# Half of h transposed by a trip through HBM and by VectorE, in a decoder layer on one core

## The chip, the cores and the metric

The kernel runs on 1 core of a Trainium2 chip. The metric is the device time of one launch in microseconds. Every time below is of the kernel before the change unless it is said otherwise.

## What is computed

One layer of a hybrid decoder: 256 tokens, width 2048, inner width 8192, all in float32. Two kinds of attention stand side by side; their heads are joined and projected back, and an MLP follows. The change touches only the passage between the last two.

```python
        mixed = jnp.concatenate([a_out.reshape(B, S, DSWA_HEADS * HEAD_DIM),
                                 b_out.reshape(B, S, MLA_HEADS * V_HEAD_DIM)], axis=-1)
        x = x + _rmsnorm(mixed @ w_out[layer], norm_attn_post[layer])

        h = _rmsnorm(x, norm_mlp_pre[layer])
        u = jnp.square(jax.nn.relu(h @ w_up[layer]))
        x = x + _rmsnorm(u @ w_down[layer], norm_mlp_post[layer])
```

Here `x` is 256 x 2048, `w_out` is 2048 x 2048, `w_up` 2048 x 8192 and `w_down` 8192 x 2048.

## The kernel before

**Numbers.** A float32 product is made from three products in a reduced type: each operand is split into `hi` (rounded, by ScalarE) and `lo` (the rest, by VectorE), and TensorE adds hi·hi, lo·hi and hi·lo. The helper `split` issues the two instructions; `split_gain` does the same and multiplies each row by its gain. So each tile of weights goes from HBM to `raw` (by SyncE's queue), then to `hi` (ScalarE), `lo` (VectorE), and to TensorE. There are 5 buffers for `raw` and 8 pairs `hi`, `lo`.

**Tokens and tiles.** The 256 tokens are two blocks of 128, block 0 and block 1. In a matmul the 128x128 stationary tile is taken from the transposed activations (rows of it are the 128 values of k over which the sum runs, columns are the tokens) and 512 columns of weights stream past. So h has to be turned: `hT` holds 16 tiles k of 128 rows, 256 tokens each, as `hT_hi` and `hT_lo`.

**From w_out to w_up.** The products with w_out are made in three passes over its columns, 512 columns to an accumulator `acc_o`. `out_evac` takes an accumulator out: ScalarE squares it (`junko`), VectorE multiplies by the gain into `yg`. When the last 512 columns of block b are there, the chain `residual(b)` starts:

- VectorE sums the squares, POOL takes the power (`rstd_post`, L506), and VectorE adds the scaled `yg` to `x` in four updates of 512 columns (`x0` and `x1` for the two blocks, L960).
- TensorE turns 512 columns at a time, in groups of four 128x128 transposes into a PSUM bank (`ht0` to `ht3`, L308). ScalarE and VectorE split each group into `hT_hi` and `hT_lo` (L314, L315). `parts[b]` counts the groups; the matmuls of tile k are put into the program only when the groups up to it are (`h_done`).
- POOL stores x in HBM with four DMAs (`xkeep`, L976). It is read again at the end of the layer.
- ScalarE takes the squares of the new x (`junkx`, L980, four of 512 columns), VectorE sums them, POOL makes `rstd_pre2`, which scales the result of w_up later. So the transposed h is the unscaled x; its gain is in the weights (`gcol`).

**The first chunk of w_up.** w_up is worked through in 8 chunks of 1024 columns; the first one (j = 0) is plain: 16 tiles of weights, 2 blocks, 2 halves of 512 columns, 3 products, hence 6 matmuls per tile and block into `acc_u0_<block><half>`. Tile k of this chunk is weight 119 + k (`hi119` is k = 0, `hi127` k = 8, `hi132` k = 13). Its order is written out: block 0 for k = 0 to 6, then block 1 for k = 0 to 6, then from k = 7 both blocks in turn.

```python
        order = in_order(len(steps), (APART[1], 0)) if j == 0 else [(t, b) for t, (w, _, _) in enumerate(steps)
        for t, b in order:
            if (j, t, b) == (0, 8, 0):
                flow.finish(*res)
                late["po"].release()
```

At (0, 8, 0), block 0 at k = 8, both residual chains have to be wholly in the program. Then the pool `po` is given back, which held `x0`, `x1`, `yg0`, `yg1` and `junk`, and in its place the pool `up` is made, with `ab`, `ab2`, `c` and others. The next chunks use products on sums of tiles; `all_sums` makes the sums of hT in `c` (with `left_sums`, on VectorE and ScalarE), and POOL and SyncE load pairs of tiles of w_up into `ab` and `ab2`. Later `c` also receives the turned inner activations.

**What sets the order.** All instructions of an engine run in the order of the program. The order is made at build time by a small planner, `Flow`: a chain such as `residual` yields a number of planned microseconds before its next piece, matmuls advance the planned clock by their cost (`flow.spend`), and `flow.pump` emits the pieces that are due. `flow.until` and `flow.finish` advance the planned clock to what they need. `D_NORM`, `D_HT` and `D_SECOND` are such delays: before the first transposes, between groups, and between the starts of the two chains.

## Time and profile before

| what | value |
|---|---|
| time, median of 3 runs | 1021.92 us (1021.72 to 1022.56) |
| the profiled execution: its time, its span | 1022.2 us, 1020.4 us |
| granted TensorE clock, mean over the span | 0.997 |
| busy: PE, PEld, DVE, ACT, POOL | 1009.9, 842.3, 841.4, 625.0, 101.1 us |
| matmuls (records) | 4670 |
| HBM read, written | 232.64 MB, 33.56 MB |
| passage concerned: last w_out products to k = 8 of both blocks | about 336 to 368 us |

PE is TensorE's matmuls, PEld its loads of stationary tiles, which overlap them; DVE is VectorE, ACT is ScalarE, POOL is GpSimd, SP is SyncE. The span goes from the first to the last instruction of the profiled execution; the time of a run also holds what lies around it. In a row of the timeline stand the start, the duration, the engine, the line of the kernel, the operation, the output and the inputs, and in brackets how long the engine had been idle before and what ended that. A row of POOLq, ACTq or SPq is a DMA being issued by that engine. Rows of DMA issues give the number, the size and the median time from issue to landing.

### The profile page before, as it was taken

To read this page: it belongs to the slowest core of one execution; us is meant where nothing else is said; L and a number is where in the kernel's file an instruction comes from. 1 tells how busy PE (TensorE), PEld (TensorE's weight loads), DVE (VectorE), ACT (ScalarE), POOL (GpSimd) and SP (SyncE) were. 2 spreads that over 40 slices of the span, in tenths; PEclk is the share of its full clock that TensorE was granted. 3 is DMA by queue.
4 is the path that set the end of the run, shared out by engine and by line. 5 is a ranking of instruction groups with operands and counts; after the bars stand their busy time and mean duration, and the time that the engine had idled before them with its cause. 6 is when DMAs were issued, how large, how long until landed. Compare 5 with 4: busy or idle time off the path is not lost.

```text
span 1020.4 us, 13299 instructions
## 1 busy us (share of the span) xinstructions
PE 1009.9 (99%) x4670; PEld 842.3 (83%) x4670; DVE 841.4 (82%) x1127; ACT 625.0 (61%) x824; POOL 101.1 (10%) x160
## 2 busy tenths in 40 slices
PE   9999999999999999999999999999999999999996
PEld 6888889898888788888888888888888888888885
DVE  6676747676666679998999989897999998898985
ACT  6575436555454567576766776676666665767661
POOL 0020302102101200000010100000110000211100
PEclk9999999999999999999999999999999999999998
DMA  8977759656687477777988979679989867888952
GB/s 291 371 250 261 245 166 309 217 175 185 207 310 208 173 298 245 258 256 241 301 264 278 286 222 295 200 253 352 338 271 391 290 234 259 296 304 333 367 187 82
DMA packets 109170, 267.07 MB, mean 262 GB/s; under 512 B 9520, under 2 KB 28464, under 8 KB 108464
## 3 DMA queue, kind: packets, MB, share of 16 engines
q1 hardware_dynamic: 65584, 175.14, 50.0%
q0 software_dynamic: 20144, 71.31, 21.1%
q10 hardware_dynamic: 23376, 19.78, 6.2%
q8 instruction: 36, 0.59, 0.2%
q14 instruction: 30, 0.25, 0.1%
HBM read 232.64 MB, written 33.56 MB: 261 GB/s over the span
## 4 chain that ended last, share of the span: by engine, by line
PE 95%; DVE 2%; issue 1%; DMA 1%; ACT 0%; POOL 0%; DVEq 0%; POOLq 0%; SPq 0%; ACTq 0%
PE acc_u L304 26%; PE y L304 25%; PE acc_o L304 8%; PE md L304 6%; PE m L304 6%; PE acc_v L304 5%; PE acc_qk L304 4%; PE acc_q L304 3%; PE acc_k L304 3%; PE acc_ckv L304 3%; PE acc_cq L304 2%; PE sc_b L304 1%; DMA raw<-in_w_in 1%; PE acc_qr L304 1%; PE y L1346 1%
## 5 line engine op out<-in xcount | busy, mean ns | idle before, releaser
L315 DVE TENSOR_TENSOR lo<-raw,hi 128x1024 fp32r<-128x1024 f32 (+2 forms) x205 | 233.4, 1157 | 65.5 <-ACT hi L314 64.1
L314 ACT ACTIVATE hi<-raw 128x1024 fp32r<-128x1024 f32 (+2 forms) x205 | 202.7, 1004 | 75.1 <-DMA raw<-in_w_in 21.8
L304 PE MATMUL acc_u<-hi,hT_lo 128*128 128x512 f32 x386 | 150.4, 390 | 0.4 <-DVE hT_lo L315 0.4
L304 PE MATMUL acc_u<-hi,hT_hi 128*128 128x512 f32 x386 | 150.7, 390 | 0.0
L304 PE MATMUL acc_u<-lo,hT_hi 128*128 128x512 f32 x386 | 150.2, 389 | 0.0
L304 PE MATMUL y<-hi,ulo 128*128 128x512 f32 x358 | 139.3, 389 | 0.0
L304 PE MATMUL y<-lo,uhi 128*128 128x512 f32 x358 | 139.3, 389 | 0.0
L304 PE MATMUL y<-hi,uhi 128*128 128x512 f32 x358 | 139.3, 389 | 0.0
L318 ACT ACTIVATE hi<-raw,gcol 128x1024 fp32r<-128x1024 f32 x86 | 96.7, 1148 | 32.6 <-PE acc_u L304 16.1
L319 DVE SCALAR_TENSOR_TENSOR lo<-raw,gcol,hi 128x1024 fp32r<-128x1024 f32 x86 | 106.5, 1272 | 9.1 <-ACT hi L318 9.1
L304 PEld LDWEIGHTS acc_u<-hi,hT_lo 128*128 128x128 f32 x386 | 72.4, 188 | 15.8 <-DVE hT_lo L315 0.9
L304 PEld LDWEIGHTS acc_u<-lo,hT_hi 128*128 128x128 f32 x386 | 72.5, 188 | 15.0
L304 PEld LDWEIGHTS acc_u<-hi,hT_hi 128*128 128x128 f32 x386 | 72.5, 188 | 14.9
L304 PEld LDWEIGHTS y<-lo,uhi 128*128 128x128 f32 x358 | 67.2, 188 | 14.1
L304 PEld LDWEIGHTS y<-hi,uhi 128*128 128x128 f32 x358 | 67.2, 188 | 14.0
L304 PEld LDWEIGHTS y<-hi,ulo 128*128 128x128 f32 x358 | 67.2, 188 | 13.9
L315 DVE TENSOR_TENSOR lo<-st_down,hi 128x1024 fp32r<-128x1024 f32 x46 | 55.0, 1218 | 0.8 <-ACT hi L314 0.8
L304 PE MATMUL acc_o<-hi,mixT_hi 128*128 128x512 f32 x128 | 51.3, 401 | 0.0
L314 ACT ACTIVATE hi<-u 128x1024 fp32r<-128x1024 f32 (+1 forms) x33 | 32.3, 980 | 30.3 <-PE y L304 12.1
L304 PE MATMUL acc_o<-hi,mixT_lo 128*128 128x512 f32 x128 | 49.9, 390 | 0.0
L304 PE MATMUL md<-hi,s 128*128 128x512 f32 x138 | 49.9, 389 | 0.0
L304 PE MATMUL acc_o<-lo,mixT_hi 128*128 128x512 f32 x128 | 49.8, 389 | 0.0
(356 smaller groups left out, 2046.9 us busy)
## 6 DMA issues: line engine op xcount, KB each, us to landing
raw<-in_w_up SPq DMA_DIRECT2D x86, 512.0 KB, 4.9
raw<-in_w_down SPq DMA_DIRECT2D x82, 512.0 KB, 6.0
raw<-in_w_in SPq DMA_DIRECT2D x55, 512.0 KB, 5.9
ab<-in_w_up POOLq DMA_DIRECT2D x17, 1024.0 KB, 7.0
raw<-in_w_out SPq DMA_DIRECT2D x32, 512.0 KB, 4.9
ab_down<-in_w_down POOLq DMA_DIRECT2D x11, 1024.0 KB, 9.3
ulo<-ukeep POOLq DMA_DIRECT2D x20, 512.0 KB, 6.7
rkeep<-r ACTq DMA_DIRECT2D x28, 256.0 KB, 3.5
```

The lines of the kernel that those rows point to most:

```text
L304: nc.tensor.matmul(out, a, b, start=start, stop=stop)
L314: nc.scalar.activation(hi, src, AF.Copy)
L315: nc.vector.tensor_tensor(out=lo, in0=src, in1=hi.bitcast(F32), op=OP.subtract)
L318: nc.scalar.activation(hi, src, AF.Copy, scale=g)
L319: nc.vector.scalar_tensor_tensor(out=lo, in0=src, scalar=g, in1=hi.bitcast(F32), op0=OP.mult, op1=OP.subtract)
L1346: nc.tensor.matmul(out, a[x], w[z], start=False, stop=(x, z) == (1, 0), skip_group_check=True)
```

## The change

The lower 1024 columns of h (k = 0 to 7) are turned by TensorE as before. The upper 1024 columns (k = 8 to 15) are not: POOL stores them in HBM (`keeph0`, `keeph1`, half a megabyte each) with the 32-column pieces put where a transpose of 32x32 blocks needs them, a DMA loads them back, VectorE turns 512 columns at a time within 32x32 blocks (L970), and the same split follows, now reading SBUF instead of PSUM. This leaves the values of k in another order within each group of 512, so the rows of w_up and the gains `norm_mlp_pre` are laid out in that order before the launch.

Block 0 and block 1 differ. Block 0's load is issued by POOL, lands in `yg0` and is turned into its second half; it is over before `po` is released. Block 1's load is issued by ScalarE's queue and lands in `c` of the new pool `up`, so it comes after the release of `po`. At (0, 8, 0) the program now needs the two `residual` chains and block 0's trip, then makes the pool, then goes on until block 1's load is issued.

Besides, delays change: 4.5 and 6.0 before the first transposes of the two blocks, 2.5 between the chains, block 0's squares 12 later, `all_sums` 10.5 later, with a shorter pause in it.

```diff
--- before.py
+++ after.py
@@ -92,7 +92,8 @@
 D_PAIR, D_KR = 3.5, 6.0
 D_LOADED, D_LATENT, D_KV = (13.0, 9.0), 3.0, (1.0, 5.0, 7.0)
 D_X0, D_X, D_SS, D_TAB = 8.0, 3.0, 3.0, (14.0, 20.0)
-D_NORM, D_HT, D_SECOND = 4.5, 1.5, 4.0
+D_NORM, D_HT, D_SECOND = (4.5, 6.0), 1.5, 2.5
+D_AWAY, D_HERE, D_GROUP, D_SQUARE = (9.0, 1.0), (9.0, 6.0), (5.0, 3.5), 12.0
 
 UP_STEP = 2.4
 
@@ -948,6 +949,30 @@
                 nc.vector.tensor_scalar_mul(xs[b][:, c], xs[b][:, c], pw[:, b:b + 1])
                 yield 1.5
 
+    fetched = []
+
+    def turn_h(b, keep):
+
+        if b:
+            while "c" not in late:
+                yield 0.5
+            back, turned = [late["c"][:, i * CW:(i + 1) * CW] for i in range(2)]
+        else:
+            back, turned = [late["yg"][b][:, i * CW:(i + 1) * CW] for i in range(2)]
+        (nc.scalar if b else nc.gpsimd).dma_start(out=back.rearrange("p (n f) -> p n f", n=2),
+                                                  in_=keep.rearrange("(n p) f -> p n f", p=P))
+        fetched.append(b)
+        yield D_HERE[b]
+        hT = late["hT"]
+        for n in (2, 3):
+            c = slice((n - 2) * 512, (n - 1) * 512)
+            tv = turned[:, c].rearrange("p (k s) -> p k s", k=4)
+            nc.vector.transpose(tv.rearrange("p k (t q) -> p k q t", q=4),
+                                back[:, c].rearrange("p (q k c) -> p k q c", q=4, k=4))
+            split(hT[0][:, 4 * n:4 * n + 4, b * P:(b + 1) * P], hT[1][:, 4 * n:4 * n + 4, b * P:(b + 1) * P], tv)
+            parts[b] += 1
+            yield D_GROUP[b]
+
     def residual(b):
 
         po, yg, hT = late["po"], late["yg"], late["hT"]
@@ -960,20 +985,32 @@
                 nc.vector.scalar_tensor_tensor(out=xs[b][:, c], in0=yg[b][:, c], scalar=r, in1=xs[b][:, c],
                                                op0=OP.mult, op1=OP.add)
 
+        def trip():
+            update((2, 3))
+            keep = dram.tile([2 * P, 512], F32, name=f"keeph{b}")
+            nc.gpsimd.dma_start(out=keep.rearrange("(g t) (q c) -> (t q) g c", g=8, q=4),
+                                in_=xs[b][:, CW:].rearrange("m (g c) -> m g c", g=8))
+            res.append(flow.start(turn_h(b, keep), D_AWAY[b]))
+
         update((0, 1))
-        yield D_NORM
-        for n in range(4):
+        if not b:
+            trip()
+        yield D_NORM[b]
+        for n in range(2):
             t = tp_bank(f"ht{n}{b}")
             for k in range(4):
                 transpose(t[:, k * P:(k + 1) * P], xs[b][:, n * 512 + k * P:n * 512 + (k + 1) * P])
             tv = t.rearrange("p (k s) -> p k s", k=4)
-            if n in (0, 1):
-                update((n + 2,))
             split(hT[0][:, 4 * n:4 * n + 4, b * P:(b + 1) * P], hT[1][:, 4 * n:4 * n + 4, b * P:(b + 1) * P], tv)
             parts[b] += 1
+            if b and not n:
+                trip()
+                yield 2.5
             yield D_HT
         for q in range(4):
             nc.gpsimd.dma_start(out=xkeep[b][32 * q:32 * q + 32], in_=xs[b][q::4, :])
+        if not b:
+            yield D_SQUARE
         for n in range(4):
             c = slice(n * 512, (n + 1) * 512)
             junk = po.tile([P, 512], BF16, tag="junk", bufs=1, name=f"junkx{n}{b}")
@@ -991,7 +1028,7 @@
     def h_done(k, b):
         flow.until(lambda: 4 * parts[b] > k)
 
-    res = [None] * NB
+    main, res = [None] * NB, []
     for ns in ((0, 1), (2,), (3,)):
         if len(ns) == 2:
             order = [(c, t, b) for ts in (range(4), range(4, 6), range(6, 8)) for c in range(2) for t in ts for b in range(NB)]
@@ -1018,7 +1055,7 @@
             if n == 3:
                 flow.finish(pw_chain)
                 weights.ahead = AHEAD_NORM
-                res[b] = flow.start(residual(b), b * D_SECOND)
+                main[b] = flow.start(residual(b), b * D_SECOND)
                 flow.pump()
     hT = late["hT"]
 
@@ -1166,7 +1203,7 @@
     def all_sums():
         for kp in range(2):
             yield from left_sums(kp)
-        yield 8.0
+        yield 2.0
         yield from left_sums(2)
 
     def three(out, a, w, first, last):
@@ -1217,14 +1254,15 @@
         for t, b in order:
             what, k, tiles = steps[t]
             if (j, t, b) == (0, 8, 0):
-                flow.finish(*res)
+                flow.finish(*main, res[0])
                 late["po"].release()
                 mix.release()
                 late["up"] = pool("up", "right")
                 late["st"] = late["up"].tile([P, ST], F32R, tag="st", bufs=1, name="st")
                 for n in ("ab", "ab2", "c", "u01"):
                     late[n] = late["up"].tile([P, 2 * CW], F32, name=n)
-                flow.start(all_sums())
+                flow.until(lambda: 1 in fetched)
+                flow.start(all_sums(), 10.5)
             if (j, t, b) == (FF // CW - 1, 4, 0):
                 weights.limit -= 1
                 u_next = split_u(0, 0)
@@ -1443,14 +1481,18 @@
     a["x"] = np.ascontiguousarray(a["x"][order])
     a["xt"] = np.ascontiguousarray(np.concatenate([a["x"], inputs["norm_attn_pre"]]).T)
     a["pos"] = np.ascontiguousarray(inputs["positions"].reshape(S)[order].reshape(NB, P).T)
-    a["gains"] = np.ascontiguousarray(np.concatenate(
-        [inputs[n].reshape(-1, P) for n in ("q_latent_norm", "kv_latent_norm", "norm_mlp_pre")]).T)
     a["w_down"] = np.ascontiguousarray(
         a["w_down"].reshape(FF // 512, 4, 4, 32, D).transpose(0, 2, 1, 3, 4).reshape(FF, D))
     q = a["w_uq"].reshape(QR, HB, NOPE + RB)
     kv = a["w_ukv"].reshape(KVR, HB, NOPE + 128)
     a["w_uq"] = np.ascontiguousarray(np.concatenate([x.reshape(QR, -1) for x in (q[:, :, :NOPE], q[:, :, NOPE:])], axis=1))
     a["w_ukv"] = np.ascontiguousarray(np.concatenate([x.reshape(KVR, -1) for x in (kv[:, :, :NOPE], kv[:, :, NOPE:])], axis=1))
+    half = a["w_up"].reshape(4, 4, 4, 32, FF)
+    a["w_up"] = np.concatenate([half[:2], half[2:].transpose(0, 2, 1, 3, 4)]).reshape(D, FF)
+    half = inputs["norm_mlp_pre"].reshape(4, 4, 4, 32)
+    pre = np.concatenate([half[:2], half[2:].transpose(0, 2, 1, 3)])
+    a["gains"] = np.ascontiguousarray(np.concatenate(
+        [g.reshape(-1, P) for g in (inputs["q_latent_norm"], inputs["kv_latent_norm"], pre)]).T)
     for n in ("norm_attn_post", "norm_mlp_post"):
         a[n] = np.ascontiguousarray(inputs[n])
     a["consts"] = shape_constants(order)
```

The order of three queues, before and now. In names like `ht01` or `junkx01` the first digit is the group of 512 columns and the second the block; in `acc_u0_01` they are the block and the half; the number behind the last underscore is a running one.

TensorE, around block 1's transposes. Before, `ht01` stands at the end of block 0's tile k = 5 and `ht11` behind k = 6 (`hi125`), ahead of block 1's first matmuls:

```order
L308 MATMUL ht01_3308<-ident_87,x1_2806 128x128 x4
L304 MATMUL acc_u0_00_3206<-hi125_3250,hT_hi_2795 128x512
L304 MATMUL acc_u0_00_3206<-lo125_3251,hT_hi_2795 128x512
L304 MATMUL acc_u0_00_3206<-hi125_3250,hT_lo_2796 128x512
L304 MATMUL acc_u0_01_3207<-hi125_3250,hT_hi_2795 128x512
L304 MATMUL acc_u0_01_3207<-lo125_3251,hT_hi_2795 128x512
L304 MATMUL acc_u0_01_3207<-hi125_3250,hT_lo_2796 128x512
L308 MATMUL ht11_3322<-ident_87,x1_2806 128x128 x4
L304 MATMUL acc_u0_10_3208<-hi119_3083,hT_hi_2795 128x512
L304 MATMUL acc_u0_10_3208<-lo119_3084,hT_hi_2795 128x512
L304 MATMUL acc_u0_10_3208<-hi119_3083,hT_lo_2796 128x512
```

Now (the rows around `ht01`, and then the ones around `ht11`):

```order
L305 MATMUL acc_u0_01_3209<-lo125_3251,hT_hi_2795 128x512
L305 MATMUL acc_u0_01_3209<-hi125_3250,hT_lo_2796 128x512
L309 MATMUL ht01_3290<-ident_87,x1_2806 128x128 x4
L305 MATMUL acc_u0_10_3210<-hi119_3083,hT_hi_2795 128x512
L305 MATMUL acc_u0_10_3210<-lo119_3084,hT_hi_2795 128x512
L305 MATMUL acc_u0_10_3210<-hi119_3083,hT_lo_2796 128x512
```

```order
L305 MATMUL acc_u0_10_3210<-hi122_3188,hT_hi_2795 128x512
L305 MATMUL acc_u0_10_3210<-lo122_3189,hT_hi_2795 128x512
L305 MATMUL acc_u0_10_3210<-hi122_3188,hT_lo_2796 128x512
L309 MATMUL ht11_3329<-ident_87,x1_2806 128x128 x4
L305 MATMUL acc_u0_11_3211<-hi122_3188,hT_hi_2795 128x512
L305 MATMUL acc_u0_11_3211<-lo122_3189,hT_hi_2795 128x512
L305 MATMUL acc_u0_11_3211<-hi122_3188,hT_lo_2796 128x512
```

`ht01` has moved behind the last matmul of block 0's k = 6 and stands right ahead of block 1's first; `ht11` has moved from there to behind 21 of block 1's matmuls, into its k = 3.

ScalarE, around block 0's upper half, from the squares of x1 on. Before:

```order
L980 ACTIVATE junkx01_3366,ssx1_2412<-x1_2806 128x512
L980 ACTIVATE junkx11_3371,ssx1_2412<-x1_2806 128x512
L980 ACTIVATE junkx21_3376,ssx1_2412<-x1_2806 128x512
L318 ACTIVATE hi127_3380<-raw127_3378,gcol_69 128x1024
L980 ACTIVATE junkx31_3387,ssx1_2412<-x1_2806 128x512
L318 ACTIVATE hi128_3399<-raw128_3397,gcol_69 128x1024
L318 ACTIVATE hi129_3405<-raw129_3403,gcol_69 128x1024
L318 ACTIVATE hi130_3411<-raw130_3409,gcol_69 128x1024
L318 ACTIVATE hi131_3423<-raw131_3421,gcol_69 128x1024
L318 ACTIVATE hi132_3435<-raw132_3433,gcol_69 128x1024
L318 ACTIVATE hi133_3463<-raw133_3461,gcol_69 128x1024
```

Now:

```order
L319 ACTIVATE hi128_3370<-raw128_3368,gcol_69 128x1024
L315 ACTIVATE hT_hi_2795<-yg0_2802 128x4x128
L1017 ACTIVATE junkx21_3380,ssx1_2412<-x1_2806 128x512
L1017 ACTIVATE junkx31_3385,ssx1_2412<-x1_2806 128x512
L319 ACTIVATE hi129_3389<-raw129_3387,gcol_69 128x1024
L319 ACTIVATE hi130_3406<-raw130_3404,gcol_69 128x1024
L319 ACTIVATE hi131_3412<-raw131_3410,gcol_69 128x1024
L319 ACTIVATE hi132_3418<-raw132_3416,gcol_69 128x1024
L962 DMA c_3442<-keeph1_3299 128x2x512
L319 ACTIVATE hi133_3447<-raw133_3445,gcol_69 128x1024
L315 ACTIVATE hT_hi_2795<-c_3442 128x4x128
```

The split of block 0's second returned group (from `yg0`) stands among the squares of x1, and the load of `c` from `keeph1` behind the split that makes `hi132`; the first split from `c` follows `hi133`.

POOL, from the first power on. Before:

```order
L506 TENSOR_TENSOR rstd_post0_3146<-t_post0_3145,neg_half_85 128x1
L976 DMA xkeep0_2421<-x0_2804 32x2048 x4
L506 TENSOR_TENSOR rstd_post1_3265<-t_post1_3264,neg_half_85 128x1
L506 TENSOR_TENSOR rstd_pre20_3296<-t_pre20_3295,neg_half_85 128x1
L976 DMA xkeep1_2422<-x1_2806 32x2048 x4
L506 TENSOR_TENSOR rstd_pre21_3394<-t_pre21_3393,neg_half_85 128x1
L379 DMA ab2_3458<-in_w_up 128x2x1024
```

Now:

```order
L507 TENSOR_TENSOR rstd_post0_3146<-t_post0_3145,neg_half_85 128x1
L991 DMA keeph0_3153<-x0_2804 128x8x128
L1011 DMA xkeep0_2421<-x0_2804 32x2048 x4
L962 DMA yg0_2802<-keeph0_3153 128x2x512
L507 TENSOR_TENSOR rstd_post1_3243<-t_post1_3242,neg_half_85 128x1
L991 DMA keeph1_3299<-x1_2806 128x8x128
L1011 DMA xkeep1_2422<-x1_2806 32x2048 x4
L507 TENSOR_TENSOR rstd_pre20_3360<-t_pre20_3359,neg_half_85 128x1
L507 TENSOR_TENSOR rstd_pre21_3398<-t_pre21_3397,neg_half_85 128x1
L380 DMA ab2_3441<-in_w_up 128x2x1024
```

The store of `keeph0` stands ahead of `xkeep0`, the load of `yg0` behind it and ahead of `rstd_post1`, and `keeph1` ahead of `xkeep1`; the powers `rstd_pre20` and `rstd_pre21` both come after those stores.

## Prediction

> **What bounds the kernel now.** I read the page first: busy times, then the chain that ended last.
>
> ```profile
> PE 1009.9 (99%) x4670; PEld 842.3 (83%) x4670; DVE 841.4 (82%) x1127; ACT 625.0 (61%) x824; POOL 101.1 (10%) x160
> PE 95%; DVE 2%; issue 1%; DMA 1%; ACT 0%; POOL 0%; DVEq 0%; POOLq 0%; SPq 0%; ACTq 0%
> 357.95 44.93 PE acc_u L304 x198
> ```
>
> TensorE is the bound from end to end. The third line, from the chain in order of time, gives its pace: 44.93 / 198 = 0.227 us for a 512-column matmul. So each microsecond taken off TensorE's queue is gained, each that its queue waits is lost, and nothing later gives it back. All that changes lies between 336 and 400 us, so next comes the timeline of that stretch, engine by engine. TensorE around the first block's transposes, the first matmul of w_up, and the start of block 1 (start us, us, engine, line, tile):
>
> ```profile
> 338.71 0.39 PE L304 MATMUL acc_o<-hi,mixT_lo 128*128 128x512 f32 x1
> 338.94 0.60 PE L308 MATMUL ht<-ident,x 128*128 128x128 f32 x4
> 339.61 0.40 PE L304 MATMUL acc_o<-lo,mixT_hi 128*128 128x512 f32 x1
> 341.92 0.39 PE L304 MATMUL acc_u<-hi,hT_hi 128*128 128x512 f32 x1
> 353.64 0.40 PE L304 MATMUL acc_u<-lo,hT_hi 128*128 128x512 f32 x1
> 354.48 0.50 PE L304 MATMUL acc_u<-hi,hT_lo 128*128 128x512 f32 x1 [0.45 <-DVE hT_lo L315]
> ```
>
> From 338.71 to 339.61 there are two matmuls and a group of four transposes: 0.90 - 2 x 0.227 = 0.45 us per group. The step from 353.64 to 354.48 is 0.84 instead of 0.23: 0.61 us lost, the only wait of TensorE in this stretch.
>
> **What is removed.** Four of eight groups of four transposes: 4 x 0.45 = 1.78 us, all on the bound. That is all there is to win, and it is below 0.2% (2.04 us), which is about the least that a measurement of this kernel can tell from no change. w_up's rows and its gains are permuted before the launch and loaded by the same instructions: nothing.
>
> **What is added for block 0** (upper half by HBM): a store keeph0, a load into yg0, two VectorE transposes, and the same two splits, which now read SBUF. It is needed at k = 8 of block 0, which stands 96 matmuls and two groups after 341.92, so not before 364. Rows for what can be late here, VectorE's updates of x0 and POOL's queue (the second line, from the groups by line, gives in its mean what it takes POOL to issue a store of this kind):
>
> ```profile
> 336.92 2.08 DVE L960 SCALAR_TENSOR_TENSOR x<-yg,rstd_post,x 128x512 f32<-128x512 f32 x3 [0.69 <-POOL rstd_post L506]
> L651 POOL DMA_DIRECT2D keep_b<-pT_b x8 | 6.1, 759 | 54.9 <-DVE pT_b L648 50.4 <-DVE lo L315 4.5
> 343.82 2.18 POOL L976 DMA_DIRECT2D xkeep<-x  x4 [6.94 <-DVE hT_lo L315]
> 349.64 0.57 POOL L506 TENSOR_TENSOR rstd_post<-t_post,neg_half 128x1 f32<-128x1 f32 x1 [3.65 <-DVE t_post L505]
> ```
>
> The store can start when the fourth update of x0 ends, 336.92 + 4 x 0.7 = 339.7. POOL now issues keeph0 (0.76), the four xkeep0 stores (2.2, to 342.7), then holds at the load of yg0 until keeph0 has landed, and only then makes rstd_post1 (0.57), for which block 1's update waits. VectorE asks for rstd_post1 at about 346.8, since two splits move ahead of it. A landing by 346 costs nothing; with 5 us (below) it is 345.5. So block 0's trip I take at zero, hidden by the 26 us before k = 8; the cover is gone if keeph0 lands later than 346, which is priced among the rivals.
>
> **What moves for block 1's lower half.** The transposes ht01 now stand right before the matmuls that read them, and ht11 three matmuls before its own. One such chain in the trace:
>
> ```profile
> 339.58 0.60 ACT L314 ACTIVATE hT_hi<-ht 128x512 fp32r<-128x512 f32 x1 [4.45 <-PE ht L308]
> 340.21 0.69 DVE L315 TENSOR_TENSOR hT_lo<-ht,hT_hi 128x512 fp32r<-128x512 f32 x1 [1.22 <-ACT hT_hi L314]
> ```
>
> From the start of the transposes (338.94): ACT after 0.64, hT_hi ready after 1.29, hT_lo after 1.96, and with the 0.05 of a semaphore the third matmul can start at 2.01. Without waiting it would start at 0.45 + 2 x 0.227 = 0.90 after ht01, and at 1.58 after ht11. So 1.11 + 0.43 = 1.54 us of waits, in place of the 0.61.
>
> **What is added for block 1** (upper half by HBM, into c): here TensorE waits. TensorE: block 0's k = 0 to 6 are 42 matmuls from 341.92, so ht01 stands at 351.45. Its third matmul is at 353.46, ht11 18 matmuls and one pace later at 357.77, the third matmul of k = 4 at 359.78, and k = 8 of block 1 is 34 further on: **367.5**.
>
> The load of c stands in ScalarE's own queue, behind the split hi132 (17 rows after ht01's). It needs the squares of x1 and block 0's second transposed group, all ahead of it there, and c lies where x0, x1 and yg lay. The prices of that queue:
>
> ```profile
> 343.80 0.59 ACT L314 ACTIVATE hT_hi<-ht 128x512 fp32r<-128x512 f32 x1
> 344.28 1.15 ACT L318 ACTIVATE hi<-raw,gcol 128x1024 fp32r<-128x1024 f32 x1
> 346.84 0.63 ACT L980 ACTIVATE junkx<-x 128x512 bf16<-128x512 f32 x1
> 347.59 0.63 ACT L980 ACTIVATE junkx<-x 128x512 bf16<-128x512 f32 x1
> 362.26 5.48 ACT L318 ACTIVATE hi<-raw,gcol 128x1024 fp32r<-128x1024 f32 x5
> L319 DVE SCALAR_TENSOR_TENSOR lo<-raw,gcol,hi 128x1024 fp32r<-128x1024 f32 x86 | 106.5, 1272 | 9.1 <-ACT hi L318 9.1
> L761 DVE STREAM_TRANSPOSE turned_kv<-mixT_hi x1: 1097/1097/1097, 190.2 to 190.2; 128x512 f32<-128x512 f32 x1
> L1063 DVE STREAM_TRANSPOSE uT<-c x16: 660/701/704, 454.6 to 586.7; 128x512 f32<-128x512 f32 x16
> ```
>
> Pace on ScalarE: hT_hi 0.48, a square with its read 0.75, a weight split hi 1.08, (5.48 - 1.15) / 4; on VectorE lo takes 1.27. A transpose on VectorE takes 0.70 or 1.10; the new ones write with the stride of the slower row, so 1.08. Stepping on: hT_hi of ht11 at 357.77 + 0.64 = 358.41, two squares, hi127 at 360.39, two squares, hi128 at 362.97 (ends 364.12). Then the second hT_hi<-yg must wait for VectorE: lo128 to 365.45, transpose to 366.5. It starts there, two squares, hi129 368.48, hi130, hi131, hi132 at 371.73. How far ahead the queue issues a DMA, and how long it then takes:
>
> ```profile
> 402.91 1.06 ACT L314 ACTIVATE hi<-ab 128x1024 fp32r<-128x1024 f32 x1 [1.82 <-PE acc_u L304]
> 403.60 0.33 ACTq L1061 DMA_DIRECT2D c<-rkeep  x1
> 403.88 1.04 ACT L314 ACTIVATE hi<-u 128x1024 fp32r<-128x1024 f32 x1
> raw<-in_w_up SPq DMA_DIRECT2D x86, 512.0 KB, 4.9
> raw<-in_w_up SPq DMA_DIRECT2D x9, 512.0 KB, 7.1
> ab<-in_w_up SPq DMA_DIRECT2D x1, 1024.0 KB, 10.1
> DMA to landing us min/median/max: 2.4/4.1/5.6
> ```
>
> The DMA leaves about when the split ahead of it starts (the split at 403.88 stands ahead of the DMA at 403.60 in the program): 371.7. A half-megabyte load lands after 4.9 us in the median of all, 7.1 between 358 and 380 us, where two 1 MB loads of ab run beside it; the quickest quarter-megabyte load of c took 2.4 (last line, four stores and four loads around 400 us). I take 4.9, since the first ab load is issued after this one, and keep 2.4 and 7.1. Landed 376.6, transposed 377.7, hT_hi 378.35, hT_lo 379.05, third matmul 379.1, against 367.5 + 0.45 = 367.95 without a wait: **11.15 us** (8.65 to 13.35). Behind the DMA stand hi133 and the later splits: their tiles are used at k = 14 and after, some 18 us on, so they are not late. SP's load of ab waits for the same stores, and is needed in the next chunk. The second transposed group of block 1 has 48 matmuls (10.9 us) of cover.
>
> **The clock after the wait.** A wait of 10 us is longer than any in the trace but its end and its start:
>
> ```profile
> 1011.79 0.39 PE L1346 MATMUL y<-hi,ulo 128*128 128x512 f32 x1
> 1014.00:1014.50 0.50, 0.00 (x0) 0.00 (x0) 0.50 (x1) 0.00 (x0) 0.00 (x0) 0.67 0.00 0
> 1014.50:1015.00 0.50, 0.00 (x0) 0.00 (x0) 0.50 (x2) 0.00 (x0) 0.00 (x0) 0.50 0.00 0
> 1.19 3.60 PE L527 MATMUL warm<-zero 128*128 128x512 bf16 x8 [1.19 <-DVE zero L524]
> 5.60 0.63 PE L304 MATMUL acc_qk<-hi,xT_hi 128*128 128x512 f32 x1
> 6.03 0.63 PE L304 MATMUL acc_qk<-hi,xT_lo 128*128 128x512 f32 x1
> 7.28 0.39 PE L304 MATMUL acc_qk<-hi,xT_hi 128*128 128x512 f32 x1
> 7.51 0.40 PE L304 MATMUL acc_qk<-hi,xT_lo 128*128 128x512 f32 x1
> ```
>
> The last matmul ends at 1012.18, and the granted clock (the figure 0.67, then 0.50) falls about 2 us later. At the start matmuls stand 0.43 us apart (5.60, 6.03) until nearly 7 us, then 0.23 (7.28, 7.51). So after the wait TensorE runs at half pace for a while: 2.3 us if only the acc_qk matmuls before 6.9 count, 5.7 us if the stretch from 1.19 does; each costs 47% of itself, 1.1 to 2.7 us. I take the middle, 1.9.
>
> [...]
>
> **The sum.** -1.78 - 0.61 + 1.54 + 11.15 + 1.9 = **+12.2 us**. Against the profiled execution's own 1022.2 us (span 1020.4) that is 1034.4; it stands 0.28 above the median of the three runs, 1021.92, so 1034.1 for the median.
>
> **Rivals.**
> 1. *Block 1's trip is hidden* (ends not slower). Then only -1.78 - 0.61 + 1.54 = -0.85 remains: 1021.1; were the waits at ht01 and ht11 hidden too, -2.4: 1019.5, just faster. It needs c landed by 367.5 - 1.1 - 0.65 = 365.7, so issued by 360.8; ScalarE's queue as stepped reaches it 11 us later, and even with no wait in it 13 instructions of 0.48 to 1.08 us lie between ht11 and the load. Chance 0.08: 0.05 within 0.2%, 0.03 faster.
> 2. *A shorter wait*, 3 to 8 us: squares or splits run ahead in TensorE's shadow, or the load lands in 2.4 us. 1025 to 1030. Against it: ScalarE idles before ht01 (347 to 352), but its queue is in order and ht01's split comes first. 0.08.
> 3. *A longer one*: the load of c shares the engines with ab and takes 10.1 (+5.2: 1039.3), or keeph0 takes 9 us, rstd_post1 comes at 350 instead of 347.4 and lo125 at 352.9 where k = 6 wants it at 350.3 (+2.6: 1036.7, with all behind it moved along). The DMA engines were idle at 339 us, which speaks against the second. 0.12.
> 4. The case forecast, 1030.5 to 1037: 0.72.
>
> **How the numbers follow.** 1034.1 is the time of case 4. The bounds of the load (-2.5, +2.2) and of the clock (-0.8, +0.8) give 1030.8 to 1037.1; to leave out no more than 2 in 10 the range takes in the upper end of case 2 and most of case 3: 1029 to 1039. Slower: 0.72 + 0.08 + 0.12 = 0.92; same 0.05; faster 0.03.
>
> **What would show it.** Right: in the waits, TensorE (acc_u) held once for some 10 us by hT_hi<-c and hT_lo<-c at about 367 us; ScalarE's load c<-keeph issued near 372; a granted clock of 0.50 in that wait; matmuls 0.43 us apart behind it; 16 transposes less; 1.1 us lost at ht01. The forecast is wrong if the load is issued before 361, or if TensorE's next work doesn't wait for it.

## The result, and the profile after

| | before | changed |
|---|---|---|
| time, median of 4 runs each | 1022.24 us | 1033.03 us (1032.38 to 1034.08) |
| ratio, 95% interval | | 1.0107 [1.0094, 1.0119] |
| the profiled execution: its time, its span | 1022.2, 1020.4 us | 1034.08, 1032.3 us |
| granted clock, mean | 0.997 | 0.993 |

The change makes the kernel 10.8 us slower by the medians and 11.9 us by the two profiled spans (the profiled run of the changed kernel is the slowest of its four). First the page of the changed kernel, busy times and the chain that ended last:

```profile
PE 1010.6 (98%) x4654; PEld 841.4 (82%) x4654; DVE 846.3 (82%) x1131; ACT 624.9 (61%) x824; POOL 104.2 (10%) x163
PE 95%; DVE 1%; ACT 1%; issue 1%; DMA 1%; DVEq 0%; POOLq 0%; POOL 0%; SPq 0%; ACTq 0%
```

16 transposes fewer (4654 against 4670), and VectorE 4.9 us busier; none of this shows where 12 us went. The waits of TensorE over the whole span (who waited, for what: us in total, times, longest) name one place; of the two waits in this row, one is of 0.7 us at ht01:

```profile
PE acc_u L305 <- ACT hT_hi L315: 10.2, 2, 9.5
```

TensorE in the changed kernel, around ht01, around block 1's k = 8, and where the spacing goes back to 0.23:

```profile
351.57 0.60 PE L309 MATMUL ht<-ident,x 128*128 128x128 f32 x4
352.86 0.50 PE L305 MATMUL acc_u<-hi,hT_hi 128*128 128x512 f32 x1 [0.69 <-ACT hT_hi L315]
353.59 0.50 PE L305 MATMUL acc_u<-hi,hT_lo 128*128 128x512 f32 x1
...
367.69 0.39 PE L305 MATMUL acc_u<-hi,hT_lo 128*128 128x512 f32 x1
377.63 0.80 PE L305 MATMUL acc_u<-hi,hT_hi 128*128 128x512 f32 x1 [9.54 <-ACT hT_hi L315]
378.22 0.63 PE L305 MATMUL acc_u<-lo,hT_hi 128*128 128x512 f32 x1
...
382.49 0.54 PE L305 MATMUL acc_u<-hi,hT_lo 128*128 128x512 f32 x1
382.86 0.40 PE L305 MATMUL acc_u<-hi,hT_hi 128*128 128x512 f32 x1
```

And the same two matmuls in the kernel before, k = 8 of block 1 and the twelfth behind it:

```profile
368.71 0.39 PE L304 MATMUL acc_u<-hi,hT_hi 128*128 128x512 f32 x1
371.43 0.39 PE L304 MATMUL acc_u<-hi,hT_hi 128*128 128x512 f32 x1
```

So the account is short. At k = 8 of block 1 the changed kernel is 377.63 - 368.71 = 8.9 us behind, twelve matmuls later 382.86 - 371.43 = 11.4, and it is still 11.5 behind at the last matmul (1023.27 against 1011.79). Some 12.2 us were lost in one wait (9.7) and in the twelve matmuls after it (2.5; they took 5.23 us instead of 2.72), and 0.8 were gained before it. The granted clock goes with the slow matmuls. The next rows are windows: start and end, length, busy us of PE, PEld, DVE, ACT and POOL, the granted clock, the DMA engines' busy share, GB/s. In the second one the clock is 0.52:

```profile
368.00:377.60 9.60, 0.08 (x1) 0.00 (x0) 7.33 (x8) 6.32 (x9) 2.23 (x2) 0.74 0.76 255
377.60:383.00 5.40, 5.37 (x13) 4.24 (x14) 4.00 (x5) 2.68 (x3) 0.00 (x0) 0.52 1.02 415
```

The timelines of ScalarE and VectorE show what TensorE waited for; the row behind them is the load's issue (count, size, us to landing):

```profile
368.28 0.18 ACT L1017 ACTIVATION_READ_ACCUMULATOR junkx<-x 128x1 f32 x1
368.37 1.13 ACT L319 ACTIVATE hi<-raw,gcol 128x1024 fp32r<-128x1024 f32 x1
368.50 0.39 ACTq L962 DMA_DIRECT2D c<-keeph  x1
369.41 4.25 ACT L319 ACTIVATE hi<-raw,gcol 128x1024 fp32r<-128x1024 f32 x4
371.06 4.86 DVE L320 SCALAR_TENSOR_TENSOR lo<-raw,gcol,hi 128x1024 fp32r<-128x1024 f32 x4
375.83 1.07 DVE L970 STREAM_TRANSPOSE c<-c 128x512 f32<-128x512 f32 x1
376.94 0.63 ACT L315 ACTIVATE hT_hi<-c 128x512 fp32r<-128x512 f32 x1 [3.28 <-DVE c L970]
```

```profile
c<-keeph ACTq DMA_DIRECT2D x1, 512.0 KB, 3.6
```

The load left at 368.50, when the last square of x1 had ended (368.46), and not behind hi132: of the splits that stand ahead of it in ScalarE's program only hi129 had started. It landed after 3.6 us, at 372.1. Then its transpose stood behind four weight splits in VectorE's queue until 375.83 (the first of the four was running at 372.1): 3.7 us in which the copy lay ready.

### The profile page after: what moved, and what is told of

It reads as the page before. It is cut to its first block, busy times and chain, and to the rows that moved or that the text cites. A ratio compares the mean times of both kernels' runs of the same rounds, so it can differ in the third digit from the quotient of the medians.

```text
span 1032.3 us, 13268 instructions
## 1 busy us (share of the span) xinstructions
PE 1010.6 (98%) x4654; PEld 841.4 (82%) x4654; DVE 846.3 (82%) x1131; ACT 624.9 (61%) x824; POOL 104.2 (10%) x163
## 4 chain that ended last, share of the span: by engine, by line
PE 95%; DVE 1%; ACT 1%; issue 1%; DMA 1%; DVEq 0%; POOLq 0%; POOL 0%; SPq 0%; ACTq 0%
PE acc_u L305 26%; PE y L305 25%; PE acc_o L305 8%; PE md L305 6%; PE m L305 6%; PE acc_v L305 5%; PE acc_qk L305 4%; PE acc_q L305 3%; PE acc_k L305 3%; PE acc_ckv L305 2%; PE acc_cq L305 2%; PE sc_b L305 1%; DMA raw<-in_w_in 1%; PE acc_qr L305 1%; PE y L1384 1%
## 5 line engine op out<-in xcount | busy, mean ns | idle before, releaser
L305 PE MATMUL acc_u<-hi,hT_hi 128*128 128x512 f32 x386 | 151.6, 393 | 10.2 <-ACT hT_hi L315 10.2
```

The lines of the kernel that those rows point to most:

```text
L305: nc.tensor.matmul(out, a, b, start=start, stop=stop)
```

## The experiments

My theory after the result was that two queues made the wait (the squares of x1 ahead of the load, VectorE's splits ahead of the transpose), and that the rest of the loss was the clock. The rivals: the late release of the pool alone, the trip through HBM itself, and, for the slow matmuls, the DMA traffic. Times are medians; "before" is the kernel before on the same chip. Unless a diff says otherwise, each edit is of the changed kernel. In the diffs, "..." stands for lines that are not shown. A wait of TensorE is put at the time at which it ends.

**yg1_late**: the copy lands in another tile, the order of the splits stays.

```diff
-D_AWAY, D_HERE, D_GROUP, D_SQUARE = (9.0, 1.0), (9.0, 6.0), (5.0, 3.5), 12.0
+D_AWAY, D_HERE, D_GROUP, D_SQUARE = (9.0, 4.0), (9.0, 8.0), (5.0, 3.5), 12.0
...
-            back, turned = [late["c"][:, i * CW:(i + 1) * CW] for i in range(2)]
...
+        back, turned = [late["yg"][b][:, i * CW:(i + 1) * CW] for i in range(2)]
-        (nc.scalar if b else nc.gpsimd).dma_start(...
+        nc.gpsimd.dma_start(...
...
-                flow.finish(*main, res[0])
+                flow.finish(*main, *res)
...
-                flow.until(lambda: 1 in fetched)
```

> Block 1's copy lands in yg1, a tile that is free as soon as x1 is updated, and POOL issues the load, so that it need not wait for the squares of x1 or the release of the pool. The order of the splits on ScalarE and VectorE is left: the transposes stand behind lo132 as before. Theory (queues): in the changed kernel the load landed at 372.1 us and its transpose waited behind four splits of VectorE until 375.8; so here the load lands before 367, the transpose still starts at about 374.7, TensorE waits 8 to 9 us, and the time is 9 to 10.5 us above the kernel before, 1031 to 1033. Rival (release): the late issue alone makes the wait; then TensorE waits 0 to 1 us and the time is 1021 to 1022.5.

Measured: 1032.62 us, ratio 1.0101 [1.0084, 1.0118]. VectorE and TensorE of this run:

```profile
370.75 3.67 DVE L320 SCALAR_TENSOR_TENSOR lo<-raw,gcol,hi 128x1024 fp32r<-128x1024 f32 x3
374.33 1.07 DVE L965 STREAM_TRANSPOSE yg<-yg 128x512 f32<-128x512 f32 x1
376.12 0.79 PE L305 MATMUL acc_u<-hi,hT_hi 128*128 128x512 f32 x1 [8.36 <-ACT hT_hi L315]
668.48 0.50 PE L305 MATMUL acc_u<-lo,hT_hi 128*128 128x512 f32 x1 [1.96 <-DVE lo L320]
```

POOL issued the load at 359.27 and it landed 4.4 us later, at 363.7; the transpose started at 374.33 all the same. So the rival of the release falls: an early copy alone is worth 1.2 us of the wait. And a new wait of 2 us stands at 668 (the last row), which the changed kernel doesn't have.

**turn_first**: the copy as in the changed kernel, but the transposes ahead of the splits.

```diff
-        if b == NB - 1:
-            weights.ahead = W_AHEAD
...
+            if (j, t, b) == (0, 4, 1):
+                weights.ahead = 2
...
                 flow.until(lambda: 1 in fetched)
+                flow.finish(*res)
+                weights.ahead = W_AHEAD
```

> Landing tile, queue and trip as in the changed kernel; weights.ahead is lowered to 2 from block 1's k = 4 on and raised again behind the transposes, so that the squares of x1 stand ahead of hi127 on ScalarE and both transposes from c ahead of lo129 on VectorE. Theory (queues): the load is issued at 364.6 to 366 us, lands 3.6 later, TensorE goes on at 370.5 to 372: a wait of 2.5 to 4 us, a half-paced stretch behind it of 0 to 2.5 us, and up to 0.7 us because hi127 comes later. The time is 2 to 6 us above the kernel before, 1024 to 1028. Rival (trip): storing, loading and turning takes that long in itself; then the wait stays above 8 us and the time is 1031 to 1034.

Measured: 1031.94 us, 1.0094 [1.0079, 1.0110], far above what was expected. The waits of TensorE:

```profile
PE acc_u L305 <- DVE lo L320: 3.1, 2, 2.5
PE acc_u L305 <- ACT hT_hi L315: 2.3, 2, 1.6
PE acc_u L305 <- DVE c L1234: 1.2, 2, 0.9
```

The place went as the theory said, and better: the load left at 363.75, the wait at k = 8 fell from 9.5 to 1.6 us, so the trip itself isn't what TensorE waited for. But new waits came, at 414 us (0.6), 436 and 437 (0.9 and 0.4) and 665 (2.5). The time did not follow the wait. (The edit also puts the splits from lo129 on behind the transposes, so this run alone does not say what makes the new waits.)

**yg1_early**: the copy in yg1, and its first transpose between lo128 and lo129.

```diff
 (as yg1_late, and weights.ahead raised only behind flow.finish(*main, *res))
...
-D_AWAY, D_HERE, D_GROUP, D_SQUARE = (9.0, 1.0), (9.0, 6.0), (5.0, 3.5), 12.0
+D_AWAY, D_HERE, D_GROUP, D_SQUARE = (9.0, 4.0), (9.0, 2.5), (9.0, 3.5), 12.0
```

> Both at once: block 1's copy lands in yg1 (load by POOL), and the first transpose of it stands between lo128 and lo129. Theory (queues): keeph1 is issued at 355.2 and lands at 359, the load lands at 363 to 367.5, the transpose starts at 365.5 to 367.5, TensorE waits 0 to 1.5 us, the clock stays up, and the time is 1020.5 to 1023. Rival (trip): the round through HBM, not the queues, is what TensorE waits for; 1028 to 1033.

Measured: 1034.87 us, 1.0124 [1.0109, 1.0139]: no faster than the changed kernel, with no wait at k = 8 at all. TensorE waited later:

```profile
PE acc_u L305 <- DVE lo L320: 4.7, 3, 2.6
PE m L305 <- DVE lo L316: 1.4, 1, 1.4
```

0.8 us at 377.9, then 1.4 at 408, 0.4 at 409.9 and 1.3 at 411.9 (the next chunk of w_up), behind which the matmuls stood 0.43 us apart until 416.7, and 2.6 at 666.7 with another such stretch. My expectation failed by 12 us: the wait at k = 8 went, and others came.

**fill**: what the clock alone costs.

```diff
+                if (j, k, b) == (0, 8, 1):
+                    idle = tp_bank("idle")
+                    for i in range(34):
+                        nc.tensor.matmul(idle, tok(hT[0], 0, 0), w[0][:, 0, 0:512], start=True, stop=True)
```

> The changed kernel with 34 matmuls of 512 columns into an unused bank (7.7 us of work that nothing reads) put into TensorE's queue right ahead of the wait for block 1's copy, so that it idles some 2 us instead of 9.5. Theory (clock): the twelve matmuls behind the wait stood 0.43 us apart because TensorE had idled; now they stand 0.23 apart, and the time falls by 2.5 us against the changed kernel, to 1030 to 1031.5. Rival (traffic): they were slow because the DMA engines moved 415 GB/s just then; then they stay 0.43 apart and the time stays at 1032.5 to 1034.

Measured: 1032.60 us, 1.0105 [1.0090, 1.0121], which is the time that was put for the rival. TensorE idled 1.85 us instead of 9.5 and still fell to half pace:

```profile
377.00 0.60 PE L305 MATMUL acc_u<-hi,hT_hi 128*128 128x512 f32 x1 [1.85 <-ACT hT_hi L315]
377.40 0.63 PE L305 MATMUL acc_u<-lo,hT_hi 128*128 128x512 f32 x1
...
380.45 0.50 PE L305 MATMUL acc_u<-hi,hT_lo 128*128 128x512 f32 x1
```

```profile
378.00:379.00 1.00, 1.00 (x4) 0.81 (x4) 0.98 (x1) 0.00 (x0) 0.00 (x0) 0.50 1.05 430
381.00:382.00 1.00, 1.00 (x6) 0.81 (x5) 0.69 (x1) 1.00 (x1) 0.00 (x0) 1.00 1.06 418
```

The last two rows are windows: the granted clock is 0.50 at 378 and 1.00 at 381, while the DMA engines move 430 and 418 GB/s in both. So here the slow matmuls follow the clock and not the traffic. But in the profiled run the fill did not keep the clock up (it fell at 377.3, just after the work had resumed), and saved only about 0.75 us of the 2.5: the twelve matmuls took 4.49 us instead of 5.23.

**apart8, tensor1, tensor0, yg1_dve**: four ways around the wait.

```diff
 apart8
...
-        order = in_order(len(steps), (APART[1], 0)) if j == 0 else ...
+        order = in_order(len(steps), (APART[1], 8)) if j == 0 else ...
 tensor1 (tensor0: 2 if b else 4, and no trip for block 0)
...
-        for n in range(2):
+        for n in range(4 if b else 2):
...
-                trip()
-                yield 2.5
+                update((2, 3))
 yg1_dve (on yg1_early, in turn_h)
...
-            split(hT[0][...], hT[1][...], tv)
+            hi, lo = [t[:, 4 * n:4 * n + 4, b * P:(b + 1) * P] for t in hT]
+            nc.vector.tensor_copy(hi, tv)
+            nc.vector.tensor_tensor(out=lo, in0=tv, in1=hi.bitcast(F32), op=OP.subtract)
```

> The changed kernel with another order of TensorE's work in the first chunk: behind k = 7, block 0 runs k = 8 to 15 and then block 1 does, so that block 1's k = 8 stands 42 matmuls (9.5 us) later. Queues and trip are left. Theory (late copy): the wait for block 1's copy is nearly covered, 0 to 1 us left at about 379 us; TensorE waits 1.5 to 2 us for lo129 at block 0's k = 10, and the clock may cost 1.7 us; the time is 1023 to 1027. Rival (backlog of the weights): once TensorE doesn't wait, VectorE, ScalarE and the loads can't keep the weights coming, and the wait moves into the next chunk; 1030 to 1035.

> Block 0's upper half goes through HBM, block 1's is turned by TensorE, in the natural order of its columns (so for these 128 tokens the rows of w_up don't match; the time is what is asked). Theory (block 1 alone): block 0's trip costs nothing, 2 groups less are -0.9 us, the waits at ht01 and ht11 about +1, and no wait at k = 8: 1020.5 to 1023. Rival (both trips): block 0's two returned groups hold ScalarE and VectorE up and cost TensorE time in this chunk or the next one; 1025 or more.

> Block 1's upper half goes through HBM as in the changed kernel, block 0's is turned by TensorE, in the natural order of its columns (for these tokens the rows of w_up don't match). Theory (queues): no group from yg0 holds ScalarE until 366.5 us, so the last square of x1 and with it the load come at about 365 instead of 368.5; the transpose from c still stands behind lo133 on VectorE, which ends about 2.5 us earlier; TensorE waits 6 to 7.5 us and runs some 5 us at half pace: 1028 to 1031. Rival (trip): the load doesn't come earlier and the time stays at 1032.5 or more.

> As yg1_early, where block 1's copy came in time and the wait at k = 8 was gone, but waits of TensorE for weights came at 406 to 412 us and later; here VectorE also makes the hi part of the four returned groups (ScalarE has no part in them). Theory (ScalarE held): in yg1_early ScalarE stood idle 2.4, 2.8 and 1.8 us for returned groups, and the splits, the raw buffers and so the loads behind them came late; without it the waits at 406 to 412 us shrink by more than half, and the time is 1021 to 1027. Rival (late release): the waits come from the pairs ab, whose memory comes free later when the copy lands in yg1; then they stay, and the time is 1031 to 1036.

| | time, us | ratio | wait at block 1's k = 8 | TensorE's later waits |
|---|---|---|---|---|
| apart8 | 1036.71 | 1.0141 [1.0124, 1.0158] | none | 4.2 at 411, 0.9 at 415, 0.6 at 426, 0.6 at 625, 2.5 at 669 |
| tensor1 | 1030.89 | 1.0087 [1.0072, 1.0102] | none | 1.5 at 409, 0.5 at 412, 0.9 at 434, 0.4 at 435, 0.9 at 621, 2.6 at 665 |
| tensor0 | 1032.67 | 1.0105 [1.0090, 1.0120] | 7.9 | none above 0.4 |
| yg1_dve | 1032.44 | 1.0098 [1.0083, 1.0113] | none | 1.4 at 407, 0.4 at 409, 1.5 at 411, 0.6 at 414, 0.8 at 436, 0.4 at 437, 2.6 at 666 |

In apart8 block 0's inner activations come back into c while the sums still use it, so these sums are of other data, and VectorE has to wait for that load:

```profile
406.14 0.69 DVE L1182 TENSOR_TENSOR c<-hT_hi,hT_lo 128x512 f32<-128x512 f32 x1 [4.83 <-DMA c<-rkeep]
```

So part of its 4.2 us at 411 is its own edit's doing, and it can't be counted for the theory or the rival. tensor0 keeps the long wait, as expected of block 1's trip; its load left at 366.33, later than the 365 I had put, and the time is 1.7 us above the range that I had put. tensor1 and yg1_dve lose the wait and are about as slow, where I had put 1020.5 to 1023 and 1021 to 1027. tensor1 has no trip for block 1 at all, so block 1's trip isn't the common cause, and with yg1_dve ScalarE's part in the returned groups isn't either. What these two kept of the change is block 0's trip and the moved work. VectorE, the first instruction of the first sums, in the kernel before and in tensor1:

```profile
372.88 0.68 DVE L1145 TENSOR_TENSOR c<-hT_hi,hT_lo 128x512 f32<-128x512 f32 x1
385.35 0.68 DVE L1181 TENSOR_TENSOR c<-hT_hi,hT_lo 128x512 f32<-128x512 f32 x1
```

The delay of 10.5 in all_sums puts some 11 us of VectorE's work 10 to 14 us later (this first piece 12.5), in front of the next chunk's splits. In the changed kernel, as I read it, TensorE's own wait covers that.

**tensor1_sums, yg1_sums, yg1_all**: the sums back in their place, on tensor1 and on yg1_early; in yg1_all also the squares of x0 and the hi parts of yg1_dve.

```diff
-        yield 2.0
+        yield 8.0
...
-                flow.start(all_sums(), 10.5)
+                flow.start(all_sums())
...
 yg1_all also: D_SQUARE = 0.0, and turn_h as in yg1_dve
```

> As tensor1 (block 0's upper half by HBM, block 1's by TensorE in the natural order of its columns, so that for these 128 tokens the rows of w_up don't match), and all_sums starts at once and pauses 8.0, as in the kernel before. Theory (sums): in tensor1 nothing was lost at k = 8, and the 9 us came from the sums, which stood on VectorE from 385 to 409 us instead of 373 to 396 and pushed the first splits of the next chunk behind TensorE's need; with them back, the waits at 407 to 435 us go, and those at 619 and 662 us if they come from the same shift: 1021 to 1025. Rival (splits): the weights' splits themselves come 6.6 us late (lo128 to lo132 end at 376 instead of 369.5), because the squares of x0 were moved behind 357 us; then waits of 3 us or more stay in the next chunk, 1026 to 1031.

> As yg1_early (both upper halves by HBM, block 1's copy in yg1 and turned ahead of lo129), and all_sums starts at once and pauses 8.0, as in the kernel before. Theory (sums): c is free at once here, so the sums run on VectorE before 400 us, TensorE's waits at 406 to 412 us shrink to under 2 us and the time is 1021 to 1026. Rival (release): the pairs ab are loaded 12 us later than in the kernel before (376.8 against 364.5 us), and their splits are what TensorE waits for; then 4 us or more of waits stay at 406 to 412 us, 1029 to 1035.

> As yg1_sums, and the squares of x0 stand where ScalarE was idle (no delay of 12 for block 0), and VectorE makes the hi part of the returned groups. Theory (sums and backlog): nothing of the change but the saved transposes is left on TensorE's queue; the splits hi129 and after come 3 to 5 us earlier than in yg1_early, no wait above 1 us is left in the next chunk, 1020 to 1023. Rival (release): as for yg1_sums, 1026 to 1033.

Measured: 1026.77 (1.0050 [1.0032, 1.0068]), 1029.40 (1.0074 [1.0058, 1.0090]) and 1025.27 us (1.0035 [1.0024, 1.0047]). In tensor1_sums every wait between 409 and 435 us is gone, and the one at 621; in yg1_sums 1.6 at 409 and 0.3 at 433 us stay of what were four waits. The first load of a pair ab, which the rivals of yg1_dve and yg1_sums blame, leaves as late with the sums moved back as without: tensor1 and tensor1_sums, and then yg1_sums, against 376.8 in yg1_early:

```profile
371.04 0.75 POOL L380 DMA_DIRECT2D ab<-in_w_up  x1 [0.45 <-ACT hi L319]
371.78 0.75 POOL L380 DMA_DIRECT2D ab<-in_w_up  x1 [0.45 <-ACT hi L319]
```

```profile
376.96 0.75 POOL L380 DMA_DIRECT2D ab<-in_w_up  x1 [4.99 <-PE acc_u L305]
```

So the late load is not what makes those waits, and the sums are shown as the cause of most of them: 4.1 us from tensor1 to tensor1_sums, 5.5 from yg1_early to yg1_sums (part of this is pace: 23 matmuls stand 0.43 apart behind the later waits of yg1_early and 7 in yg1_sums). The squares of x0 and the hi parts together are worth another 4.1, from yg1_sums to yg1_all; they were not tried apart. All three times are above what was expected, by 1.8, 3.4 and 2.3 us, and above the kernel before, and the three share one wait. TensorE's waits in yg1_all and that wait in tensor1_sums, then VectorE at one instruction shortly ahead of it, in the kernel before, in yg1_all and in tensor1_sums:

```profile
PE acc_u L305 <- DVE lo L320: 3.6, 3, 2.6
659.49 0.50 PE L305 MATMUL acc_u<-lo,hT_hi 128*128 128x512 f32 x1 [2.48 <-DVE lo L320]
```

```profile
642.80 0.69 DVE L371 TENSOR_TENSOR u<-u,ab 128x512 f32<-128x512 f32 x1
```

```profile
646.32 0.69 DVE L372 TENSOR_TENSOR u<-u,ab 128x512 f32<-128x512 f32 x1
```

```profile
646.45 0.69 DVE L372 TENSOR_TENSOR u<-u,ab 128x512 f32<-128x512 f32 x1
```

VectorE comes to this instruction 3.5 us later in yg1_all and 3.7 in tensor1_sums, some 240 us after anything that was changed. A window of the kernel before shows why it can stay late so long (the third busy time is DVE's):

```profile
500.00:550.00 50.00, 50.00 (x222) 41.43 (x221) 47.25 (x53) 34.51 (x40) 4.01 (x5) 1.00 0.88 280
```

VectorE is busy 94% of that window, and 93% from 385 to 655 us. Hence the last experiment.

**four_more**: the kernel before, and four such transposes on VectorE that nothing reads.

```diff
...
         for kp in range(2):
             yield from left_sums(kp)
+        for i in range(4):
+            tv = late["c"][:, 1024 + i % 2 * 512:1536 + i % 2 * 512].rearrange("p (k s) -> p k s", k=4)
+            nc.vector.transpose(tv.rearrange("p k (t q) -> p k q t", q=4),
+                                late["c"][:, 0:512].rearrange("p (q k c) -> p k q c", q=4, k=4))
         yield 8.0
...
```

> The kernel before (all of h turned by TensorE, no trip), with four VectorE transposes of the new kind added that nothing reads (4 x 1.08 = 4.3 us), right behind the second pair of sums, at about 385 us. Nothing else is moved. Theory (VectorE has no slack): VectorE is busy 94% of 385 to 655 us, keeps the lateness that it is given there, and TensorE waits for it, 2.5 to 4.4 us in all, partly at 400 to 420 us, partly at about 655 us where yg1_all waited 2.6; the time is 1024 to 1026.5. Rival (VectorE is hidden): TensorE is the only bound, the 5% of idle time take the 4.3 us up, no new wait above 0.5 us, 1021.5 to 1022.5.

Measured: 1024.70 us against 1021.83, 1.0030 [1.0018, 1.0042]. VectorE's four transposes, the instruction of above, and TensorE:

```profile
385.91 3.84 DVE L1171 STREAM_TRANSPOSE c<-c 128x512 f32<-128x512 f32 x4
645.09 0.69 DVE L371 TENSOR_TENSOR u<-u,ab 128x512 f32<-128x512 f32 x1
645.70 1.22 DVE L315 TENSOR_TENSOR lo<-ab,hi 128x1024 fp32r<-128x1024 f32 x1
658.14 0.50 PE L304 MATMUL acc_u<-lo,hT_hi 128*128 128x512 f32 x1 [1.25 <-DVE lo L319]
```

3.84 us of work at 386 us make a wait at 658 us. (The lo behind the updates, 645.70 here, starts at 643.41 in the kernel before: 2.3 us of the 3.84 were carried that far.) The time is as expected; the waits are not: this one, of 1.25 us, is half of the least that I had put, and none came at 400 to 420. It is most of the 1.9 us by which the spans differ; the rest of the medians' 2.9 is not traced. Shown: VectorE has too little slack in the up-projection to take four more transposes for nothing. No version beat the kernel before.

## Why the prediction came out

**Right in the time, and in where it is lost.** TensorE waits for block 1's copy at k = 8, the wait and the half-paced matmuls behind it are all that the changed kernel loses, and nothing later gives them back. By the steps: the third matmul behind ht01 stands 2.02 us after the transposes (353.59 - 351.57), put at 2.01; block 1's k = 8 would have come at 367.92 (367.69 and one pace), put at 367.5 (the 367.95 of the prediction is the third matmul there). Up to that place the change gains 0.8 us (367.92 against 368.71), put at 0.85. Block 0's trip cost no wait in the changed kernel: TensorE's two waits were at ht01 and at block 1's k = 8. But the zero holds only beside the long wait: tensor1_sums has block 0's trip, the moved squares and no trip for block 1, and is 4.9 us slower than the kernel before.

**Right in sum, wrong in its terms.** The wait of 11.15 was 9.7 (377.63 - 367.92) at the first matmul, inside the bounds; the prediction counted it at the third, where it is 10.3, but the 0.6 between them is part of the 2.5 of the clock below. So the sum came out as -0.8 + 9.7 + 2.5 = 11.4, against -0.85 + 11.15 + 1.9 = 12.2. Three steps of the wait were off and nearly cancelled:

- "The DMA leaves about when the split ahead of it starts", 371.7. It left at 368.50, with the end of the last square (368.46), three splits ahead of it in the program unstarted. turn_first (363.75, the last square ended at 363.73) and tensor0 (366.33, at 366.30) show the same: in these runs it goes with the end of the squares. So the issue of this load wasn't held to the place that it has in ScalarE's program; what lets it go ahead of the three splits, no run here shows.
- Landing 4.9; it took 3.6 (4.7 in tensor0).
- The transpose was taken to start at the landing. It waited 3.7 us in VectorE's queue behind four splits. The prediction stepped ScalarE's queue and never VectorE's behind the load: this is the step that failed, and it hid the other two. The load came 3.2 us earlier than put, its landing took 1.3 less, and the queue added 3.7: that the transpose started within 0.8 us of the 376.6 that was put is luck.

**The clock.** 1.9 was put; twelve matmuls at 0.43 cost 5.23 - 2.72 = 2.5, near the upper bound of 2.7.

**Wrong: "each microsecond taken off TensorE's queue is gained", and with it rival 1.** It gave 1021.1 us were the trip hidden. yg1_early and yg1_dve hid it, tensor1 left it out, and they took 1031 to 1035. The changed kernel holds more costs, which its wait covers: the sums that stand later on VectorE, shown by tensor1_sums and yg1_sums, and lateness of VectorE that lasts to about 660 us. Its added transposes alone make such lateness (four_more: 2.9 us by the medians, 1.9 by the spans); how much of it in the changed kernel is theirs is open. The removed 1.78 us of TensorE can't pay for that. "They are not late", said of the splits behind the load, held in a kernel where TensorE stood still: in yg1_early, where it did not, it waited 0.8 us for a weight split that stands behind the transposes (at 377.9).

**Open.** In yg1_all VectorE is 3.5 us late at 646 us and TensorE waits 2.6; four added transposes made 2.3 and 1.3 of these in four_more. But the count of transposes is not the measure: tensor1_sums has two more instead of four, no hi parts on VectorE, and is as late (3.7 us, a wait of 2.5). What else makes VectorE late (the time that it idles for returned groups, the moved squares, in yg1_all the four hi parts of 0.43 us each) was not separated. Nor was it tried to give VectorE's work to POOL, which is 10% busy.

## What to carry to other kernels

When a change takes work from the engine that bounds and gives it to another, look at the other one's share of busy time in the stage that follows, not in the stage of the change: in this kernel an engine at 94% kept 2.3 of 3.84 us of lateness for 260 us and handed it back at a tight place. Step every queue that the moved data passes, including the one that receives it: here the landed copy stood 3.7 us behind four splits of VectorE. And when a long wait is removed, price what it was covering before you count it as gained.

## What the runs showed that was not expected

- The clock fell behind short waits too. In turn_first TensorE idled 1.64 us, ran 1.5 us at full pace, and then the clock fell to 0.50 (370.8 to 374.2). In fill it fell to 0.50 behind 1.85 us of idling (377.3 to 380.7). An idle time of 2.56 us was followed by half pace in tensor1 (665.7 to 669.1) and left the clock at 1.00 in yg1_all (at 657 to 659). In the changed kernel it fell 4.4 us after the last matmul (372.5). So in these runs the length of the wait alone does not tell whether the clock drops; what else does was not tried. The stretches at 0.50 in these runs had nearly one length, or two or three times that: 3.4 us in turn_first, fill, tensor1 and yg1_sums, 6.8 twice in yg1_early, 10.2 in the changed kernel (372.5 to 382.8) and in tensor0.
- A load of half a megabyte into SBUF took 3.6 us from ScalarE's queue in a busy stretch, against 8.3 us for the same load issued by POOL for block 0 at 344.7 us. The issuing engine is not the reason: POOL's load in yg1_late, at 359.27, took 4.4.
- A conversion of 128x512 to the reduced type took VectorE 0.43 us (in yg1_all, from yg1), against 0.63 on ScalarE for the same piece (in the changed kernel, at 376.94).
